# Strassen blocks for the up-projection of a gated MLP, with the down-projection as a phase of its own

## The chip, the cores and the metric

The kernel runs on one core of a Trainium2 chip. The metric is the device time of one execution in microseconds (us). Inputs and outputs lie in HBM; the work runs on TensorE (matrix products), VectorE, ScalarE and GpSimd (elementwise work), and on DMA queues, which SyncE issues here. TensorE's products accumulate in PSUM, and everything else lies in SBUF, 128 partitions wide. In the rows of the profile TensorE is PE, its weight load PEld, VectorE DVE, ScalarE ACT, GpSimd POOL and SyncE SP.

## The reference

One layer of a streaming encoder on 1024 tokens of 1024 channels, in float32. Only the last part is touched by the change:

```python
proj = einsum('btd,dc->btc', h, w_in)            # 1024 -> 2560 columns
mix = concat([pool_mixer(...), hgrn2_mixer(...)]) @ w_out
h = layer_norm(ALPHA * h + mix, ln1_g, ln1_b)    # 1024 tokens x 1024
u = einsum('btd,df->btf', h, w_up)               # 1024 -> 2 * 2816
uc = conv_b + sum(conv_w[j] * pad(u)[:, j:j + T] for j in range(3))
a, v = split(uc, 2)
ffn = einsum('btf,fd->btd', gelu(a) * v, w_down) # 2816 -> 1024
h = layer_norm(ALPHA * h + ffn, ln2_g, ln2_b)
```

## The kernel before

Every large product is done in three passes. An operand r is split into a high part h (a copy in the format F32R, by ScalarE) and a low part r - h (a subtraction, by VectorE): this is `split`, lines 66 to 68. `mm3` (lines 84 to 87) then issues three matmuls, high x high, high x low, low x high, into the same place of PSUM. Line 67 is thus every high part, line 68 every low part, and lines 85 to 87 nearly all matmuls. A matmul has a 128x128 stationary operand and a moving one of 128x512.

Weights come by `weight` (line 73): a DMA of 128x1024 values (512 KB) on SyncE's queue into one of three buffers `raw`, then a split into one of five pairs `wh`, `wl`. PSUM is cut into four units of 128x1024 (`unit`, line 56); each has two halves of 512 columns.

The kernel runs in stages: the input projection with the two mixers woven into it; the output projection with the first norm; the gated MLP; the second norm. The arrays `bh` and `bl` [channel, token] hold the operand of each stage in high and low parts, 8 channel tiles of 128 x 1024 tokens. The weights `w_out` with k from 5 on lie in a pool of their own (`woh`, `wol`).

**Output projection and first norm (lines 500 to 535).** Eight token tiles of 128 tokens: the first three share each arriving row of weights, the others follow one by one. For each tile VectorE adds the residual out of PSUM (line 530) and takes statistics (line 485), and `layer_norm` forms the normed state in `z[t]`, which stays in SBUF for the residual of the second norm. `hidden(t)` transposes the tile by eight TensorE transposes into a unit of PSUM (line 515), and ScalarE and VectorE write it as high and low part into `bh`, `bl` (lines 518, 519). The last two tiles are transposed inside the first feature block of the up-projection.

**Gated MLP (lines 542 to 620).** The 2816 features are 22 blocks f of 128. For a block, `up_pair` makes the a tile and the v tile of `w_up`, each as two token halves of 8 channel tiles x 3 matmuls. Then come the convolution over tokens (ScalarE's pass with scale and bias, line 550, and two steps of VectorE, line 554, for each of a and v), GELU, the product, and a split into `gh`, `gl`, which are the stationary operands of the down-projection. `down` takes a group of blocks (`GRP`: nine of two, one of four): for each of eight token tiles it adds up the group's blocks in PSUM, and VectorE adds the result to `z[t]` (lines 601, 603). The down-projection of a group is issued after the first block of the next group, so that TensorE has work while a group's gated blocks are made. The last group ends in the second norm (lines 591 and 608).

**What sets the order.** The framework gives each engine one queue, in which it places the instructions while building; their order can differ from that of the code, since an instruction that is ready early is moved forward. At run time each engine works its queue in order, and an instruction waits for semaphores of other engines or of DMA queues. A read or a write of a tile waits for what touched it last on another engine; a unit of PSUM is one tile, with both its halves.

Of the kernel before, what the change touches and what calls it, by code (L numbers as in the profile page):

```python
# [682 lines left out]
```

## Time and profile before

| | |
|---|---|
| time, median of 3 runs | 1122.4 us (1122.37 to 1122.55) |
| span of the profiled execution | 1121.3 us |
| its own time | not recorded apart from its span |
| mean granted TensorE clock | 0.997 |
| TensorE busy | 1108.6 us, 5076 matmuls in the trace |
| VectorE busy | 641.0 us |
| ScalarE busy | 301.4 us |
| moved by DMA | 65.65 MB |

The span runs from the first to the last instruction, the time of a run also covers what lies around it. A busy time is the union of an engine's instructions; where several matmuls are under way at once it counts them once. The granted clock is a share of TensorE's full speed, 2.4 GHz; 0.50 is its lower level of 1.2 GHz.

### The profile page before, as it was taken

To read this page: it belongs to the slowest core of one execution; us is meant where nothing else is said; L and a number is where in the kernel's file an instruction comes from. 1 tells how busy PE (TensorE), PEld (TensorE's weight loads), DVE (VectorE), ACT (ScalarE), POOL (GpSimd) and SP (SyncE) were. 2 spreads that over 40 slices of the span, in tenths; PEclk is the share of its full clock that TensorE was granted. 3 is DMA by queue.
4 is the path that set the end of the run, shared out by engine and by line. 5 is a ranking of instruction groups with operands and counts; after the bars stand their busy time and mean duration, and the time that the engine had idled before them with its cause. 6 is when DMAs were issued, how large, how long until landed. Compare 5 with 4: busy or idle time off the path is not lost.

```text
span 1121.3 us, 11896 instructions
## 1 busy us (share of the span) xinstructions
PE 1108.6 (99%) x5076; PEld 916.7 (82%) x5076; DVE 641.0 (57%) x668; ACT 301.4 (27%) x314; POOL 59.0 (5%) x71
## 2 busy tenths in 40 slices
PE   9999999999999999999999999999999999999996
PEld 7888888888888888888888888888888888888874
DVE  6585498677756744635354453535445453454388
ACT  5422433324500232122221212213131221313211
POOL 2000000011011100000000000000000000000025
PEclk9999999999999999999999999999999999999998
DMA  8200111101321411021111102111110211111012
GB/s 314 93 1 29 47 57 38 39 19 48 116 70 51 149 58 57 22 73 38 57 57 38 57 19 76 38 57 57 38 57 19 75 38 57 41 54 37 1 57 94
DMA packets 19205, 65.65 MB, mean 59 GB/s; under 512 B 2128, under 2 KB 3024, under 8 KB 19152
## 3 DMA queue, kind: packets, MB, share of 16 engines
q1 hardware_dynamic: 19008, 64.82, 17.4%
q8 instruction: 40, 0.66, 0.2%
q14 instruction: 13, 0.11, 0.0%
q10 hardware_dynamic: 144, 0.07, 0.0%
HBM read 60.68 MB, written 4.19 MB: 58 GB/s over the span
## 4 chain that ended last, share of the span: by engine, by line
PE 95%; POOL 2%; DVE 1%; ACT 0%; DMA 0%; issue 0%; POOLq 0%; DVEq 0%
PE u L85 30%; PE u L86 30%; PE u L87 30%; PE u L228 2%; POOL z L465 1%; POOL rs L448 1%; PE u L268 1%; PE u L515 1%; PE u L270 1%; PE u L257 1%; DVE z L480 0%; ACT z L462 0%; DVE st L485 0%; POOL rs L449 0%; PE u L195 0%; PE u L196 0%
## 5 line engine op out<-in xcount | busy, mean ns | idle before, releaser
L85 PE MATMUL u<-bh,wh 128*128 128x512 f32 x960 | 375.6, 392 | 0.6 <-ACT bh L67 0.6
L86 PE MATMUL u<-bl,wh 128*128 128x512 f32 x960 | 374.5, 390 | 0.0
L87 PE MATMUL u<-bh,wl 128*128 128x512 f32 x960 | 374.3, 390 | 0.0
L68 DVE TENSOR_TENSOR wl<-raw,wh 128x1024 fp32r<-128x1024 f32 x88 | 107.1, 1229 | 285.6 <-ACT wh L67 283.2
L85 PEld LDWEIGHTS u<-bh,wh 128*128 128x128 f32 x960 | 180.6, 188 | 38.4 <-ACT bh L67 1.1
L86 PEld LDWEIGHTS u<-bl,wh 128*128 128x128 f32 x960 | 180.7, 188 | 37.7 <-DVE bl L68 0.8
L87 PEld LDWEIGHTS u<-bh,wl 128*128 128x128 f32 x960 | 180.6, 188 | 37.8
L67 ACT ACTIVATE wh<-raw 128x1024 fp32r<-128x1024 f32 x88 | 92.1, 1059 | 389.0 <-PE u L86 259.2
L85 PE MATMUL u<-wh,gh 128*128 128x512 f32 x352 | 139.3, 396 | 0.0
L87 PE MATMUL u<-wh,gl 128*128 128x512 f32 x352 | 139.2, 396 | 0.0
L86 PE MATMUL u<-wl,gh 128*128 128x512 f32 x352 | 139.2, 395 | 0.0
L603 DVE TENSOR_TENSOR z<-u,z 128x1024 f32<-128x1024 f32 x64 | 78.3, 1224 | 57.5 <-PE u L87 57.5
L85 PEld LDWEIGHTS u<-wh,gh 128*128 128x128 f32 x352 | 66.1, 188 | 16.2 <-ACT gh L67 0.3
L86 PEld LDWEIGHTS u<-wl,gh 128*128 128x128 f32 x352 | 66.1, 188 | 16.0
L87 PEld LDWEIGHTS u<-wh,gl 128*128 128x128 f32 x352 | 66.1, 188 | 15.9
L554 DVE SCALAR_TENSOR_TENSOR cv<-u,pkt,cv 128x1023 f32<-128x1023 f32 (+4 forms) x46 | 56.7, 1232 | 9.3 <-ACT cv L550 8.8
L448 POOL TENSOR_SCALAR rs<-mv 128x1 f32<-128x1 f32 x16 | 17.5, 1093 | 799.0 <-DVE mv L456 799.0
L554 DVE SCALAR_TENSOR_TENSOR ca<-u,pkt,ca 128x1023 f32<-128x1023 f32 (+4 forms) x46 | 56.7, 1233 | 2.2 <-ACT ca L550 1.4
L85 PE MATMUL u<-wh,bh 128*128 128x512 f32 x144 | 57.6, 400 | 0.0
L86 PE MATMUL u<-wl,bh 128*128 128x512 f32 x144 | 56.2, 390 | 0.0
L87 PE MATMUL u<-wh,bl 128*128 128x512 f32 x144 | 56.2, 390 | 0.0
L67 ACT ACTIVATE gh<-ca 128x1024 fp32r<-128x1024 f32 (+1 forms) x23 | 23.6, 1025 | 104.4 <-DVE ca L578 104.4
(123 smaller groups left out, 949.1 us busy)
## 6 DMA issues: line engine op xcount, KB each, us to landing
raw<-in_w_up SPq DMA_DIRECT2D x44, 512.0 KB, 3.5
raw<-in_w_down SPq DMA_DIRECT2D x22, 512.0 KB, 3.5
raw<-in_w_ct SPq DMA_DIRECT2D x13, 512.0 KB, 3.4
raw<-in_w_out SPq DMA_DIRECT2D x8, 512.0 KB, 3.5
raw<-in_x SPq DMA_DIRECT2D x8, 512.0 KB, 3.9
hg<-in_xT SPq DMA_DIRECT2D x7, 512.0 KB, 8.1
out<-z SPq DMA_DIRECT2D x6, 512.0 KB, 2.6
raw<-in_w_i SPq DMA_DIRECT2D x4, 512.0 KB, 5.2
```

What stands on the lines that cost most here:

```text
L67: A.activation(out=h, in_=r, func=AF.Copy)
L68: V.tensor_tensor(out=l, in0=r, in1=h.bitcast(F32), op=ALU.subtract)
L85: PE.matmul(o, lhsT=ah, rhs=bh, start=start, stop=False)
L86: PE.matmul(o, lhsT=ah, rhs=bl, start=False, stop=False)
L87: PE.matmul(o, lhsT=al, rhs=bh, start=False, stop=stop)
L228: PE.matmul(ul[:, p * P:(p + 1) * P], lhsT=km[:, p * P:(p + 1) * P], rhs=view(QF, p * P + hh, [2 * hh, 64 // hh], [512 - hh, 2], [1, hh]), ...
L257: PE.matmul(up[:, c * P:(c + 1) * P], lhsT=KTr[:, c * P:(c + 1) * P], rhs=vchunk(c, hs), start=True, stop=True)
L268: PE.matmul(uo[:, cs], lhsT=vchunk(c, hs), rhs=sc[:, cs], start=True, stop=c == 0)
L270: PE.matmul(uo[:, cs], lhsT=S[:, (c - 1) * P:c * P], rhs=QF[:, cs], start=False, stop=True)
L448: G.tensor_scalar(out=rs, in0=mv[:, 1:2], scalar1=LN_EPS, scalar2=None, op0=ALU.add)
L554: V.scalar_tensor_tensor(out=c[:, o], in0=u[:, i], scalar=pkt[:, cw + j:cw + j + 1], in1=c[:, o], op0=ALU.mult, op1=ALU.add)
L603: V.tensor_tensor(out=z[t], in0=u, in1=z[t], op=ALU.add)
```

## The change

The first norm, the up-projection and the down-projection are rebuilt.

**The products.** For each feature block f the up-projection is a 2x2 block product: rows are the a tile and the v tile of the weights, the inner dimension is the two halves of the channels (four channel tiles each), and the columns are the two token halves. A form of Strassen's scheme makes it from seven block products of 4 channel tiles x 3 matmuls each: "11", "12", "s1", "s2", "s3", "22", "s4" (`pair`). Their weight operands are blocks of the weights or sums of them, formed in `prep` (two loads, four half-width sums, three full-width splits and one half-width split). Their token operands are the first token half as it is (in `bh`, `bl`), and for the second half four combinations T1 to T4 and B22, formed in `hidden` from the transposed tile t and the tile t - 4 of the first half, which is kept in `fh`. T1 and B22 lie in the second token half of `bh`, `bl`; T2, T3, T4 in new arrays `th`, `tlo`.

**The accumulation.** A block uses two units of PSUM with the halves c1, c2 and c3, c4. c1 takes "11", is copied by ScalarE, takes "s2" on top, is copied, takes "s3" on top, is copied. c3 takes "s1", is read, and takes "s4" on top. VectorE adds the copies to c2, c3 and c4 and so makes the tiles a and v in SBUF. `post` does the convolution, GELU and the product on these.

**The phases.** The up-projection of all 22 blocks comes first: in `step`, the block f, the convolution of block f - 1 and the weights of block f + 1 go side by side. The product goes to HBM (`gd`), and the normed state too (`hd`); the output projection takes the token tiles in the order 0, 4, 1, 5, 2, 3, 6, 7, and tile 6 is transposed ahead of the last channel tile of tile 7. Then the down-projection runs as a phase of its own, in groups of 2, 4, 4, 4, 4 and 4 blocks: weights and gated blocks are loaded and split, the latter into `bh`, `bl`, the former into `wh`, `wl` or, for f % 10 from 5 on, into the pairs `dh`, `dl` of a new pool. The second norm is as before.

The core of the diff (`parts` cuts a split weight into its two channel halves, `blocks` regards a transposed tile as 8 or 4 tiles of 128, `step` advances each generator; `first_group` brings the operands of the first group while the last block runs):

```diff
-GRP = (2,) * 9 + (4,)
+GRP = (2,) + (4,) * 5
...
+    hd = [tc.dram_tile([P, D], F32, name=f"hd{t}") for t in range(NC)]
+    gd = [tc.dram_tile([P, T], F32, name=f"gd{f}") for f in range(NF)]
+    tpp = tc.tile_pool(name="tpp", bufs=1, reuse_waits="tile")
+    tp = tpp.__enter__()
+    th, tlo = (tp.tile([P, 3, 4, 512], F32R, name=n) for n in ("th", "tlo"))
...
+    first_half = {}
     def hidden(t):
         ut = unit()
         for k in range(KT):
             PE.transpose(out=ut[:, k * P:(k + 1) * P], in_=z[t][:, k * P:(k + 1) * P], identity=identt)
-        ut3 = ut.rearrange("p (k t) -> p k t", t=P)
         ts = slice(t * P, (t + 1) * P)
-        A.activation(out=bh[:, :, ts], in_=ut3, func=AF.Copy)
-        V.tensor_tensor(out=bl[:, :, ts], in0=ut3, in1=bh[:, :, ts].bitcast(F32), op=ALU.subtract)
+        if t < 4:
+            split(blocks(ut), bh[:, :, ts], bl[:, :, ts])
+            r = zp.tile([P, 1024], F32, tag="fh", name="fh", bufs=2)
+            A.activation(out=r, in_=ut, func=AF.Copy)
+            first_half[t] = r
+            return
+        r = first_half.pop(t - 4)
+        d = rawp.tile([P, 1024], F32, tag="raw", name="rawd")
+        s = slice(ts.start - 512, ts.stop - 512)
+        V.tensor_tensor(out=d[:, lo], in0=r[:, lo], in1=ut[:, lo], op=ALU.subtract)
+        A.activation(out=r[:, lo], in_=ut[:, lo], func=AF.Copy)
+        V.scalar_tensor_tensor(out=d[:, hi], in0=ut[:, hi], scalar=-1.0, in1=d[:, lo], op0=ALU.mult, op1=ALU.subtract)
+        split(blocks(d[:, hi]), th[:, 0, :, s], tlo[:, 0, :, s])
+        split(blocks(d[:, lo]), bh[:, 0:4, ts], bl[:, 0:4, ts])
+        V.tensor_tensor(out=r[:, lo], in0=ut[:, hi], in1=r[:, lo], op=ALU.subtract)
+        split(blocks(r[:, lo]), th[:, 1, :, s], tlo[:, 1, :, s])
+        V.tensor_tensor(out=r[:, hi], in0=r[:, hi], in1=d[:, hi], op=ALU.add)
+        split(blocks(r[:, hi]), th[:, 2, :, s], tlo[:, 2, :, s])
+        split(blocks(ut[:, hi]), bh[:, 4:8, ts], bl[:, 4:8, ts])
+    def norm1(u, t):
+        z[t] = zp.tile([P, D], F32, tag="z", name="z")
+        nc.sync.dma_start(out=z[t], in_=x[t])
+        V.scalar_tensor_tensor(out=z[t], in0=z[t], scalar=ALPHA, in1=u, op0=ALU.mult, op1=ALU.add)
+        st6 = small.tile([P, 2, 6], F32, tag="st6", name="st6")
+        for c in halves:
+            stats(z[t], c, st6)
+        layer_norm(z[t], g1, b1_, st6, "whole", hd[t])
     late = []
-    for tl in ((0, 1, 2), (3,), (4,), (5,), (6,), (7,)):
+    for tl in ((0, 4, 1), (5,), (2,), (3,), (6,)):
         us = [unit() for t in tl]
         out_proj(us, tl)
-        while late and late[0] < tl[-1] - 1:
+        while len(late) > 1:
             hidden(late.pop(0))
         late += tl
         for u, t in zip(us, tl):
-            V.scalar_tensor_tensor(out=z[t], in0=xr, scalar=ALPHA, in1=u, op0=ALU.mult, op1=ALU.add)
-            layer_norm(z[t], g1, b1_, st6, "whole")
+            norm1(u, t)
+    hidden(late.pop(0))
+    u7 = unit()
+    out_proj([u7], (7,), (7, lambda: hidden(late.pop(0))))
+    norm1(u7, 7)
     wop.__exit__(None, None, None)
+    def prep(f):
+        ra, rv = raw(w_up[f]), raw(w_up[NF + f])
+        w = wpair()
+        split(ra, *w)
+        o = ops[f] = {}
+        o["11"], o["12"] = parts(w)
+        yield
+        s1 = ua.tile([P, 512], F32, tag="s1", name="s1")
+        V.tensor_tensor(out=s1, in0=rv[:, lo], in1=rv[:, hi], op=ALU.add)
+        V.tensor_tensor(out=rv[:, lo], in0=ra[:, lo], in1=rv[:, lo], op=ALU.add)
+        yield
+        V.tensor_tensor(out=ra[:, lo], in0=s1, in1=ra[:, lo], op=ALU.add)
+        V.tensor_tensor(out=ra[:, hi], in0=ra[:, lo], in1=ra[:, hi], op=ALU.add)
+        yield
+        w = wpair()
+        split(ra, *w)
+        o["s2"], o["s4"] = parts(w)
+        yield
+        w = wpair()
+        split(rv, *w)
+        o["s3"], o["22"] = parts(w)
+        yield
+        o["s1"] = [ua.tile([P, 512], F32R, tag=f"w1{n}", name=f"w1{n}", bufs=1) for n in "hl"]
+        split(s1, *o["s1"])
+    def prod(o, w, b, start, stop):
+        for k in range(4):
+            ks = slice(k * P, (k + 1) * P)
+            mm3(o, w[0][:, ks], w[1][:, ks], b[0][:, k, :], b[1][:, k, :], start and k == 0, stop and k == 3, skip_group_check=True)
+    def block(k, n):
+        return [e[:, k * 4:(k + 1) * 4, halves[n]] for e in (bh, bl)]
+    B11, T1, B21, B22 = block(0, 0), block(0, 1), block(1, 0), block(1, 1)
+    T2, T3, T4 = [[e[:, i] for e in (th, tlo)] for i in range(3)]
+    def pair(f):
+        w = ops[f]
+        a, v = outs[f] = [ua.tile([P, T], F32, tag=f"u{n}", name=f"u{n}") for n in "av"]
+        u = unit()
+        c1, c2 = u[:, lo], u[:, hi]
+        prod(c1, w["11"], B11, True, False)
+        A.activation(out=a[:, lo], in_=c1, func=AF.Copy)
+        yield
+        prod(c2, w["12"], B21, True, True)
+        V.tensor_tensor(out=a[:, lo], in0=c2, in1=a[:, lo], op=ALU.add)
+        yield
+        prod(c1, w["s2"], T2, False, False)
+        A.activation(out=a[:, hi], in_=c1, func=AF.Copy)
+        yield
+        u = unit()
+        c3, c4 = u[:, lo], u[:, hi]
+        prod(c3, w["s1"], T1, True, False)
+        yield
+        prod(c1, w["s3"], T3, False, True)
+        A.activation(out=v[:, lo], in_=c1, func=AF.Copy)
+        V.scalar_tensor_tensor(out=v[:, hi], in0=c3, scalar=-1.0, in1=v[:, lo], op0=ALU.mult, op1=ALU.subtract)
+        yield
+        prod(c4, w["22"], T4, True, True)
+        V.tensor_tensor(out=v[:, lo], in0=c4, in1=v[:, lo], op=ALU.subtract)
+        yield
+        prod(c3, w["s4"], B22, False, True)
+        V.tensor_tensor(out=a[:, hi], in0=c3, in1=a[:, hi], op=ALU.add)
...
+    def post(f):
+        a, v = outs.pop(f)
+        cv, ca = (ug.tile([P, T], F32, tag=f"c{n}", name=f"c{n}") for n in "va")
+        conv(cv, v, NF + f)
+        yield
+        yield
+        conv(ca, a, f)
+        yield
+        A.activation(out=ca, in_=ca, func=AF.Gelu_apprx_tanh)
+        yield
+        V.tensor_tensor(out=ca, in0=ca, in1=cv, op=ALU.mult)
+        nc.sync.dma_start(out=gd[f], in_=ca)
+    preps = [prep(f) for f in range(NF)]
+    step([preps[0]], 6)
+    step([preps[1]])
+    pairs = [pair(0), pair(1)]
+    step(pairs[:1], 2)
+    step(pairs[1:])
+    hidden(7)
+    step(pairs[1:])
     g2, b2 = row(2, "g"), row(3, "b")
...
+    step([pairs[0], preps[1]], 6)
+    step([pairs[1], post(0), preps[2]], 6)
+    for f in range(2, NF - 1):
+        step([pair(f), post(f - 1), preps[f + 1]], 7)
+    def down_weight(f):
+        if f % 10 < 5:
+            wd[f] = weight(w_down[f])
+            return
+        r = raw(w_down[f])
+        wd[f] = [dn.tile([P, 1024], F32R, tag=f"d{n}", name=f"d{n}") for n in "hl"]
+        split(r, *wd[f])
+    def gated(f):
+        r = raw(gd[f])
+        split(r, bh[:, f % 8, :], bl[:, f % 8, :])
...
+    for p in (post(NF - 2), post(NF - 1)):
+        step([p], 6)
+    tpp.__exit__(None, None, None)
+    zq = ctx.enter_context(tc.tile_pool(name="zq", bufs=1, reuse_waits="tile"))
+    dn = ctx.enter_context(tc.tile_pool(name="dn", bufs=5, side="right", reuse_waits="tile"))
+    z = [zq.tile([P, D], F32, name=f"z{t}") for t in range(NC)]
+    for t in range(NC):
+        nc.sync.dma_start(out=z[t], in_=hd[t])
+    for gi, fs in enumerate(groups):
+        last = gi == len(groups) - 1
+        ahead = [] if last else list(groups[gi + 1])
         for t in range(NC):
             ts = slice(t * P, (t + 1) * P)
-            last = gi == len(GRP) - 1
...
-                for i, (gh, gl) in enumerate(gs):
-                    mm3(u[:, c], gh[:, ts], gl[:, ts], ws[i][0][:, c], ws[i][1][:, c], i == 0, i == len(gs) - 1)
+                for f in fs:
+                    mm3(u[:, c], bh[:, f % 8, ts], bl[:, f % 8, ts], wd[f][0][:, c], wd[f][1][:, c], f == fs[0], f == fs[-1])
                 if last and t >= SPLIT:
                     drain(u, c)
             if not last:
                     V.scalar_tensor_tensor(out=z[t], in0=z[t], scalar=ALPHA, in1=u, op0=ALU.mult, op1=ALU.add)
                 else:
                     V.tensor_tensor(out=z[t], in0=u, in1=z[t], op=ALU.add)
+                if ahead:
+                    f = ahead.pop(0)
+                    down_weight(f)
+                    gated(f)
```

**Order of TensorE's queue in the middle of the up-projection.** `u_...` are units of PSUM. Before, one block (`u_3151` is its a tile, `u_3152` its v tile) and the first rows of the next one behind it:

```order
L85 MATMUL u_3151<-bh_82,wh_3141 128x512 [waits DVE_49]
L86 MATMUL u_3151<-bl_83,wh_3141 128x512
L87 MATMUL u_3151<-bh_82,wl_3142 128x512
...
L85 MATMUL u_3152<-bh_82,wh_3147 128x512 [waits DVE_49]
...
L85 MATMUL u_3275<-bh_82,wh_3265 128x512 [waits DVE_49]
...
L85 MATMUL u_3276<-bh_82,wh_3271 128x512 [waits DVE_49,Activation_49]
```

After, one block (`u_3416` holds c1 and c2, `u_3477` c3 and c4; `w1h` is the high part for s1), with the next block's first unit `u_3547`; each row left out belongs to the product of the row above it:

```order
L85 MATMUL u_3416<-bh_82,wh_3308 128x512 [waits Activation_49]
...
L85 MATMUL u_3477<-bh_82,w1h_3397 128x512
...
L85 MATMUL u_3416<-th_2017,wh_3360 128x512 [waits DVE_49]
...
L85 MATMUL u_3477<-bh_82,w1h_3397 128x512
...
L85 MATMUL u_3547<-bh_82,wh_3439 128x512
L85 MATMUL u_3416<-th_2017,wh_3380 128x512 [waits Activation_49]
...
L86 MATMUL u_3547<-bl_83,wh_3439 128x512
...
L85 MATMUL u_3477<-th_2017,wh_3380 128x512 [waits DVE_49]
...
L87 MATMUL u_3547<-bh_82,wl_3440 128x512
...
L85 MATMUL u_3477<-bh_82,wh_3360 128x512 [waits DVE_49]
...
L85 MATMUL u_3547<-bh_82,wh_3439 128x512 [waits Activation_49]
```

Before, one wait stood in front of 48 matmuls of one accumulation. Now the products of a block alternate with those of its other unit and of the next block, and five rows of a block wait for VectorE or ScalarE.

**Order of VectorE's queue between output projection and up-projection.** `wl_2624` and `wl_2630` are the low parts of the first a and v tile of `w_up`, `z6` and `z7` the last two token tiles. Before:

```order
L68 TENSOR_TENSOR wl_2624<-raw_2621,wh_2623 128x1024 [waits DMAHW6_49,Activation_49]
L476 SCALAR_TENSOR_TENSOR z6_1991<-z6_1991,mv_2530,row0_1996 128x1024 [waits DVE_49]
L68 TENSOR_TENSOR wl_2630<-raw_2627,wh_2629 128x1024 [waits DMAHW7_49,Activation_49]
L480 SCALAR_TENSOR_TENSOR z6_1991<-z6_1991,rs_2532,row1_1998 128x1024 [waits DVE_49,Pool_49]
...
L530 SCALAR_TENSOR_TENSOR z7_1992<-raw_2597,u_2537 128x1024 [waits DMAHW5_49,PE_49]
L519 TENSOR_TENSOR bl_83<-u_2586,bh_82 128x8x128 [waits Activation_49]
L485 BN_STATS st6_2600<-z7_1992 128x6 [waits DVE_49]
L485 BN_STATS st6_2600<-z7_1992 128x6
L68 TENSOR_TENSOR wl_2894<-raw_2891,wh_2893 128x1024 [waits DMAHW2_49,Activation_49]
```

After (`wl_2717` is the low part of the first a tile, `u_2663` the transposed tile 6, `z_2694` the token tile 7):

```order
L547 TENSOR_TENSOR rawd_2672<-fh_2591,u_2663 128x512 [waits PE_49,Activation_49]
L549 SCALAR_TENSOR_TENSOR rawd_2672<-u_2663,rawd_2672 128x512 [waits Activation_49]
L68 TENSOR_TENSOR bl_83<-rawd_2672,bh_82 128x4x128 [waits Activation_49]
L552 TENSOR_TENSOR fh_2591<-u_2663,fh_2591 128x512
L68 TENSOR_TENSOR tlo_2018<-rawd_2672,th_2017 128x4x128 [waits Activation_49]
L554 TENSOR_TENSOR fh_2591<-fh_2591,rawd_2672 128x512
L561 SCALAR_TENSOR_TENSOR z_2694<-z_2694,u_2620 128x1024 [waits DMAHW3_49,DMAHW0_49,PE_49]
L68 TENSOR_TENSOR tlo_2018<-fh_2591,th_2017 128x4x128 [waits Activation_49] x2
L68 TENSOR_TENSOR bl_83<-u_2663,bh_82 128x4x128 [waits Activation_49]
L498 BN_STATS st6_2697<-z_2694 128x6 [waits DVE_49]
L498 BN_STATS st6_2697<-z_2694 128x6
L68 TENSOR_TENSOR wl_2717<-raw_2712,wh_2716 128x1024 [waits DMAHW5_49]
```

The low part of the first weight stood among the norms of tile 6; now it stands behind the nine half-width operations of the transposed tile 6, the residual add of tile 7 and its statistics.

**Order of SyncE's queue at the end of the up-projection.** Before, with loads for both projections in alternation:

```order
L63 DMA raw_5495<-in_w_up 128x1024 [waits DMAHW3_49,DVE_49]
L63 DMA raw_5501<-in_w_up 128x1024 [waits DMAHW4_49,DVE_49]
L63 DMA raw_5619<-in_w_down 128x1024 [waits DMAHW5_49,DVE_49]
L63 DMA raw_5625<-in_w_down 128x1024 [waits DMAHW6_49,DVE_49]
L63 DMA raw_5743<-in_w_up 128x1024 [waits DMAHW7_49,DVE_49]
```

After (`gd20` and `gd21` are the last two gated blocks, `hd` the normed state in HBM):

```order
L674 DMA gd20_2012<-ca_5626 128x1024 [waits DVE_49]
L63 DMA raw_5734<-in_w_down 128x1024 [waits DMAHW5_49,DVE_49]
L63 DMA raw_5740<-gd4_1996 128x1024 [waits DMAHW7_49,DMAHW2_49,DVE_49]
L737 DMA z0_5656<-hd0_1984 128x1024 [waits PE_49]
L737 DMA z1_5657<-hd1_1985 128x1024 [waits Pool_49]
...
L737 DMA z7_5663<-hd7_1991 128x1024 [waits DMAHW2_49]
L674 DMA gd21_2013<-ca_5637 128x1024 [waits DMAHW3_49,DVE_49]
L63 DMA raw_5758<-in_w_down 128x1024 [waits DMAHW4_49,Activation_49]
```

The loads of the normed state stand as one run of eight between the stores of the last two gated blocks, and in front of the loads for the groups that follow.

## Rows read from the trace of the kernel before

**Rows 1.** The page: busy time, share, instructions; then the chain of waits by engine.

```profile
PE 1108.6 (99%) x5076; PEld 916.7 (82%) x5076; DVE 641.0 (57%) x668; ACT 301.4 (27%) x314; POOL 59.0 (5%) x71
...
PE 95%; POOL 2%; DVE 1%; ACT 0%; DMA 0%; issue 0%; POOLq 0%; DVEq 0%
```

**Rows 2.** Stretches: us, busy (x) of PE, PEld, DVE, ACT, POOL; clock, DMA share, GB/s.

```profile
600.00:700.00 100.00, 100.00 (x440) 82.17 (x439) 45.68 (x39) 23.36 (x22) 0.00 (x0) 1.00 0.17 53
```

**Rows 3.** Groups by line, shapes apart: busy us, mean ns of one | idle before, releasers.

```profile
L85 PE MATMUL u<-bh,wh 128*128 128x512 f32 x960 | 375.6, 392 | 0.6 <-ACT bh L67 0.6
...
L68 DVE TENSOR_TENSOR wl<-raw,wh 128x1024 fp32r<-128x1024 f32 x88 | 107.1, 1229 | 285.6 <-ACT wh L67 283.2 <-PE u L228 2.4
...
L67 ACT ACTIVATE wh<-raw 128x1024 fp32r<-128x1024 f32 x88 | 92.1, 1059 | 389.0 <-PE u L86 259.2 <-PE u L87 122.0 <-DMA raw<-in_w_up 6.0
...
L554 DVE SCALAR_TENSOR_TENSOR cv<-u,pkt,cv 128x1022 f32<-128x1022 f32 x21 | 26.9, 1279 | 0.4
...
L240 DVE TENSOR_TENSOR hg<-hg,hg 128x512 f32<-128x512 f32 x28 | 19.2, 687 | 19.9 <-PE u L228 19.7
...
L591 DVE TENSOR_TENSOR z<-u,z 128x512 f32<-128x512 f32 x16 | 10.5, 678 | 0.7 <-PE u L87 0.7
...
L302 ACT ACTIVATE tmp<-u 128x512 f32<-128x512 f32 x8 | 4.4, 590 | 0.2 <-PE u L87 0.2
...
L554 DVE SCALAR_TENSOR_TENSOR ca<-u,pkt,ca 128x512 f32<-128x512 f32 x2 | 1.5, 751 | 1.5 <-ACT ca L550 1.4
```

**Rows 4.** Timeline from 600 us: start, us, engine, line, operation [idle before, releaser].

```profile
599.84 0.40 PE L87 MATMUL u<-wh,gl 128*128 128x512 f32 x1
...
601.24 0.40 PE L87 MATMUL u<-wh,gl 128*128 128x512 f32 x1
...
601.67 1.23 DVE L603 TENSOR_TENSOR z<-u,z 128x1024 f32<-128x1024 f32 x1 [1.57 <-PE u L87]
...
605.64 0.39 PE L85 MATMUL u<-bh,wh 128*128 128x512 f32 x1
...
615.16 0.39 PE L85 MATMUL u<-bh,wh 128*128 128x512 f32 x1
```

**Rows 5.** Timeline from 384 us, VectorE behind the output projection.

```profile
384.40 1.22 DVE L519 TENSOR_TENSOR bl<-u,bh 128x1024 fp32r<-128x1024 f32 x1
...
385.53 1.28 DVE L485 BATCH_NORM_STATS2 st<-z 128x6 f32<-128x512 f32 x2
...
386.72 1.21 DVE L68 TENSOR_TENSOR wl<-raw,wh 128x1024 fp32r<-128x1024 f32 x1
```

**Rows 6.** Timeline from 388 us: TensorE starting again, and the last transposed tile.

```profile
388.88 0.19 PEld L85 LDWEIGHTS u<-bh,wh 128*128 128x128 f32 x1
...
389.22 0.40 PE L86 MATMUL u<-bl,wh 128*128 128x512 f32 x1
...
395.52 1.03 ACT L518 ACTIVATE bh<-u 128x1024 fp32r<-128x1024 f32 x1 [5.30 <-PE u L515]
...
396.58 1.23 DVE L519 TENSOR_TENSOR bl<-u,bh 128x1024 fp32r<-128x1024 f32 x1 [4.04 <-ACT bh L518]
...
396.60 0.30 PEld L85 LDWEIGHTS u<-bh,wh 128*128 128x128 f32 x2 [0.39 <-ACT bh L518]
```

**Rows 7.** Stretches of 1 us at the end, with columns as in rows 2.

```profile
1110.00:1111.00 1.00, 0.21 (x1) 0.00 (x0) 0.97 (x3) 0.00 (x0) 0.92 (x2) 1.00 0.94 381
1114.00:1115.00 1.00, 0.00 (x0) 0.00 (x0) 1.00 (x2) 0.00 (x0) 1.00 (x1) 0.92 0.55 209
1115.00:1116.00 1.00, 0.00 (x0) 0.00 (x0) 0.80 (x1) 0.00 (x0) 0.92 (x3) 0.50 0.15 53
```

**Rows 8.** Timeline from 0 us: matmuls before the clock is up.

```profile
7.81 0.63 PE L86 MATMUL u<-bl,wh 128*128 128x512 f32 x1
...
8.24 0.63 PE L87 MATMUL u<-bh,wl 128*128 128x512 f32 x1
```

**Rows 9.** The page: DMA issues, count, KB each, median us from issue to landing.

```profile
raw<-in_w_down SPq DMA_DIRECT2D x22, 512.0 KB, 3.5
```

More of the change, by code (lines that the diff above doesn't have):

```diff
@@ L498, in out_weight, with out_proj @@
         return h, l
-    def out_proj(us, tl):
+    def out_proj(us, tl, at=None):
         for k in range(KT):
+            if at is not None and k == at[0]:
+                at[1]()
             if w_rows[k] is None:
@@ L582, in down, with parts @@
-    def down(gi, fs, gs):
-        ws = [weight(w_down[f]) for f in fs]
+            norm1(u, t)
[3 more added lines that the diff above has]
+    norm1(u7, 7)
+    wop.__exit__(None, None, None)
+    uap = tc.tile_pool(name="uap", bufs=2, side="right", reuse_waits="tile")
+    ua = uap.__enter__()
+    ops, outs = {}, {}
+    lo, hi = halves
+    def parts(w):
+        return [[e[:, c] for e in w] for c in halves]
+    def prep(f):
[22 more added lines that the diff above has]
+        split(s1, *o["s1"])
@@ new lines, in conv @@
+    def conv(c, u, ft):
+        cw = PK_CW + 3 * ft
+        A.activation(out=c, in_=u, func=AF.Identity, scale=pkt[:, cw + 2:cw + 3], bias=pkt[:, PK_CB + ft:PK_CB + ft + 1])
+        for j in (1, 0):
+            V.scalar_tensor_tensor(out=c[:, 2 - j:], in0=u[:, :T - 2 + j], scalar=pkt[:, cw + j:cw + j + 1], in1=c[:, 2 - j:], op0=ALU.mult, op1=ALU.add)
+    def post(f):
[10 more added lines that the diff above has]
+        nc.sync.dma_start(out=gd[f], in_=ca)
@@ new lines, in step @@
+    def step(gens, n=1):
+        for i in range(n):
+            for g in gens:
+                next(g, None)
+    preps = [prep(f) for f in range(NF)]
[6 more added lines that the diff above has]
+    step(pairs[1:])
+    zpp.__exit__(None, None, None)
+    ugp = tc.tile_pool(name="ugp", bufs=2, reuse_waits="tile")
+    ug = ugp.__enter__()
+    g2, b2 = row(2, "g"), row(3, "b")
+    step([pairs[0], preps[1]], 6)
@@ new lines, in block_kernel @@
+    step([pairs[1], post(0), preps[2]], 6)
+    for f in range(2, NF - 1):
+        step([pair(f), post(f - 1), preps[f + 1]], 7)
+    groups, f0 = [], 0
+    for n in GRP:
+        groups.append(list(range(f0, f0 + n)))
+        f0 += n
+    wd = [None] * NF
+    def down_weight(f):
[5 more added lines that the diff above has]
+        split(r, *wd[f])
@@ new lines, in gated, with first_group @@
+    def gated(f):
+        r = raw(gd[f])
+        split(r, bh[:, f % 8, :], bl[:, f % 8, :])
+    def first_group():
+        for f in groups[0]:
+            down_weight(f)
+            yield
+        for i in range(3):
+            yield
+        for f in groups[0]:
+            gated(f)
+            yield
+    step([pair(NF - 1), first_group()], 7)
+    for p in (post(NF - 2), post(NF - 1)):
+        step([p], 6)
+    ugp.__exit__(None, None, None)
+    tpp.__exit__(None, None, None)
+    uap.__exit__(None, None, None)
```

72 lines of the change are left out of this document (12 added, 60 removed).

## The prediction

> **What bounds the kernel now.** I read the busy table first: TensorE is busy for 99% of the span, VectorE for 57%, ScalarE for 27%, and the chain of waits that ended last lies on TensorE for 95% [rows 1]. The table of stretches says the same of the MLP: in a stretch of 100 us that holds both projections TensorE never rests, VectorE works 46 us and ScalarE 23 us, the DMA engines are used to 17%, at the full granted clock, the upper of its two levels, 2.4 GHz [rows 2]. So a matmul taken out is time taken out, unless the engines that feed it come late. The size of the gain is not in the table of groups, though: its mean of 392 ns for a matmul [rows 3] is from entry to exit, and several are under way at once. The timeline gives what one costs. In the up-projection the starts at 605.64 and 615.16 lie 42 matmuls apart: 0.2267 us each [rows 4]. In the down-projection the starts at 599.84 and 601.24 lie six apart: 0.2333 us [rows 4].
>
> **Matmuls.** A feature block (one a tile and one v tile; there are 22) takes 2 tiles x 2 token halves x 8 channel tiles x 3 = 96 matmuls now, and 7 products x 4 x 3 = 84 after. The down-projection keeps its 48 per block. Which pitch holds for the new operands no row shows. In the built programs the operands of the slower rows (gh, gl) start 32 bytes past a multiple of 64, those of the faster ones (wh, wl, bh, bl) on a multiple. By that, as an estimate, the s1 product (12 of 84, weights w1h, w1l) and the down weights dh, dl (10 of 22 blocks) run at 0.2333, the rest, th and tlo too, at 0.2267. Before: 22 x 96 x 0.2267 + 22 x 48 x 0.2333 = 478.8 + 246.4 = 725.2 us. After: 22 x (72 x 0.2267 + 12 x 0.2333) + 480 x 0.2333 + 576 x 0.2267 = 420.7 + 242.6 = 663.3. That is **-61.9 us**; -47.7 if all ran at the slower pitch, -66.9 if all at the faster. The transposes stay 64.
>
> **The work beside it.** Per block VectorE gets three full-width splits (1229 ns), one half-width split and four half-width sums (687), three adds out of PSUM (678) and one scalar_tensor_tensor (751), four taps of the convolution (1279) and the product (1.22 as a split): 16.3 us by durations [rows 3]. Neighbours overlap: starts at 384.40, 385.53 and 386.72 are 1.13 apart for a full-width operation of 1.22 and 1.19 for two half-width ones of 0.64 [rows 5], about 0.09 less for each of 17 operations: 14.7 us. A block lasts 84 matmuls, 19.1 us, so VectorE fits, with 4 us to spare. ScalarE has 8.5 full-width passes, at the 1059 ns of a high part [rows 3] 9 us. The 60 added transfers of 512 KB land in about 3.5 us each [rows 9] on DMA engines that are mostly free, and weights are loaded a block ahead. All this is hidden as long as the order of the queues fits, which is the next point.
>
> **Four short waits in each block.** Both halves of a unit of PSUM count as one tile: s2 waits until VectorE has read c2, s3 until ScalarE has copied c1, 22 until VectorE has read c3 (after ScalarE's copy), s4 until it has read c4. The built order puts matmuls of other products into these gaps: 9, 4, 7 and 4. The lags, from rows: a matmul ends 0.39 after it starts; the reader starts 0.03 later (601.24 + 0.40, then 601.67) [rows 4]; after ScalarE's end at 396.55 VectorE starts at 396.58 and TensorE at 396.60 [rows 6]; a pipeline that was stopped takes 0.34 from the first weight load to the second matmul (388.88 to 389.22), 0.11 more than the pitch [rows 6]. Counted from the start of the last matmul before the gap:
> - s4: 0.39 + 0.03 + 0.68 + 0.05 = 1.15 against 5 pitches, 1.13: with the restart 0.13 late.
> - 22: 0.39 + 0.03 + 0.59 (half-width ScalarE copy [rows 3]) + 0.03 + 0.75 + 0.05 = 1.84 against 8 pitches, 1.81: 0.14 late.
> - s3: 1.06 against 1.15: in time.
> - s2: the read of c2 stands in VectorE's queue behind seven operations. Counted from the last matmul of 22 of the block before: 1.10 (the read of c4) + 1.13 (split) + 0.2 (ScalarE's pass) + 3 x 1.19 (taps) + 2 x 0.60 (sums) + 0.59 + 0.68 = 8.5. TensorE arrives after 1.13 + 0.13 (s4), 24 x 0.2267 and 9 x 0.2333, at 8.8. In time, by 0.3.
>
> Sum 0.27 a block, some 20 blocks: **+6**. No row shows such a loop. Below, 0: the order covers all. Above: VectorE at its full durations ends the read of c2 0.6 later and one late wait pushes the next, 1.2 a block, 26 us. I take 6, since each term is nearest to the rows in which nothing else runs.
>
> **From the output projection to the up-projection.** Now VectorE does 1.2 us for each transposed tile after the first norm; after, a tile of the second token half costs it nine half-width operations, each behind a ScalarE pass. In the new order tile 6 is transposed six matmuls before the output projection ends. Behind it in VectorE's queue stand those nine, the residual add of tile 7 and two statistics, and only then the low split of the first up weight. Added up with the ScalarE passes between them, from the end of the transposes: 2.2 for two sums with ScalarE's copy between, 2.4 for two low splits and two sums, 1.1 for the add, 1.8 for three low splits, 1.2 for the statistics, 1.2 for the weight's own split: the low part is there at 9.9. ScalarE's high part is there at 4.0. TensorE has six matmuls (1.4 us) and two more from 4.0 on: idle for 2.7 + 5.4 = 8.1 us. Then c2 waits for the copy of c1 (0.85, nothing stands between), pair 1 for its high weight at the end of three ScalarE passes behind VectorE's last sum (2.8), and its own c2 again 0.85. Together 12.6 us; before, TensorE waited 0.4 there [rows 6]. In the idle 5.4 us the clock may fall: after the last matmul (to 1110.21) the granted clock is still 0.92 in 1114 to 1115 and 0.50, the lower level of 1.2 GHz, from 1115 [rows 7]. Matmuls at that level start 0.43 apart (7.81, 8.24) [rows 8]; ten of them cost 2.0 more, of which the 2.8 us of waiting for pair 1 hide nearly all. I take **+13**. Bounds: 8 (nothing but the low split is late) and 17 (the clock stays low for the two next products).
>
> **From the up- to the down-projection.** The normed state comes back from HBM into the room of th and tlo, so its first load waits for product 22 of the last block. In SP's queue it stands behind two loads (wd4, gd4) and the store of gd20, which wait for VectorE, but ahead of the store of gd21. It is issued 0.2 us after that product, lands 3.5 later, and is needed only when the fifth token tile wants a free unit of PSUM, 11 us on. Added up the same way from the last product of block 20, the gated blocks 2 to 5 are split by 42 us, and TensorE comes for the last at 43. That is close; I add **+1** for the order of 22 and v, which waits behind a split (0 to 5).
>
> **The end.** The last group still has four blocks and the same norms; VectorE comes to it without the splits of the last gated block: **-0.5** (-2 to 0).
>
> **Sum.** -61.9 + 6 + 13 + 1 - 0.5 = -42.4. The profiled execution has a span of 1121.3 and the runs a median of 1122.4; what lies around the span (1.1) stays, so the change is taken off the median: **1080 us**.
>
> **Rivals.**
> 1. The loops bind. VectorE works at its full durations, the wait for c2 becomes the longest of each block, 26 us instead of 6: 1100. For it: VectorE goes from 46% busy to nearly 80%, in order, with ScalarE in the loop. Against it: 4 us to spare per block.
> 2. Nothing is late but the first low split: 0 for the loops, 8 for the first join, 0 for the second: 1068. For it: the order was laid so that other products fill each gap. Against it: sums of rows exceed two of the four gaps.
> 3. Slower than before: the short stops bring the clock down. If in a block all 84 matmuls started 0.43 apart, it would cost 84 x 0.203 = 17.1 us; from 2.5 of the 22 blocks on, the 42 us are gone, and with every other block it is 1080 + 11 x 17.1 = 1268 us. Against it: the granted clock is full for 4 us after the last matmul [rows 7], and these stops are a fifth of a microsecond. The Trainium skill ("TensorE: Matmul & The Clock Gate", section "A second HAM failure mode: psum-queue depth-cycling") says that frequent micro-idles between groups of matmuls, while units of PSUM are cycled, can make the clock oscillate; by that rule the change loses, and no run here shows stops of this kind.
>
> That the matmuls are not removed is excluded: TensorE's program has 4461 rows instead of 4726.
>
> **How the numbers follow.** The forecast has 0.54 (its own range 1072 to 1091), rival 1 0.23, rival 2 0.17, rival 3 0.05; 0.01 is left for sums of delays that just meet the gain. The range goes from rival 2 to a little beyond rival 1: 1066 to 1105. A measurement tells 0.2% from no change, 2.2 us, which only the last two cases come near: faster 0.94, same 0.01, slower 0.05.
>
> **What would show it.** Right: 1848 up matmuls in the trace; a pitch of 0.227 inside a product; blocks of 19.3 to 19.7 us; one hole of 7 to 10 us on TensorE near 385, ended by the low split of the first up weight, and some 3 us soon after; full clock in the up-projection; no wait for the loads of z. Wrong: blocks above 20.3 us (rival 1); a granted clock of 0.50 in the up-projection (rival 3); an idle TensorE at the second join, ended by a DMA or by a split of a gated block.

## The result and the profile after

The changed kernel takes 1082.1 us (median of 4 runs, 1081.6 to 1083.2) against 1122.5 us for the kernel before: a ratio of 0.964, 95% interval 0.963 to 0.965. The forecast was 1080, with 1072 to 1091 as its own range.

The page's busy times, and the chain of waits by engine, for [rows 1]:

```profile
PE 1059.0 (98%) x4812; PEld 863.7 (80%) x4812; DVE 761.6 (70%) x882; ACT 387.3 (36%) x444; POOL 57.0 (5%) x71
...
PE 91%; DVE 3%; POOL 2%; ACT 1%; DMA 1%; issue 1%; POOLq 0%; DVEq 0%; ACTq 0%
```

TensorE still sets the end; it has 264 matmuls fewer, and VectorE 121 us more work. The stretches (columns as in [rows 2]) show where TensorE is not busy:

```profile
385.00:390.00 5.00, 0.73 (x2) 0.30 (x2) 5.00 (x9) 2.81 (x5) 0.00 (x0) 0.85 0.30 105
390.00:395.00 5.00, 2.73 (x7) 2.18 (x8) 5.00 (x8) 0.63 (x1) 1.99 (x2) 0.50 0.00 0
395.00:405.00 10.00, 8.51 (x38) 6.10 (x36) 8.77 (x12) 4.69 (x7) 0.00 (x0) 0.98 0.60 211
440.00:780.00 340.00, 340.00 (x1466) 270.79 (x1465) 266.50 (x298) 153.26 (x176) 0.00 (x0) 1.00 0.25 81
```

From 385 to 395 us, between output projection and up-projection, TensorE is busy for 3.5 us while VectorE never rests, and the granted clock goes to its lower level, 0.50. From 440 to 780 TensorE counts as busy all the time at the full clock, and VectorE has 266.5 of 340 us, 78%.

The first join in the timeline (start, length, engine, line, operation, idle time before and what ended it):

```profile
383.41 0.39 PE L87 MATMUL u<-woh,bl 128*128 128x512 f32 x1
...
386.22 0.50 PE L85 MATMUL u<-bh,wh 128*128 128x512 f32 x1 [2.42 <-ACT wh L67]
...
386.56 0.40 PE L86 MATMUL u<-bl,wh 128*128 128x512 f32 x1
...
391.00 1.21 DVE L68 TENSOR_TENSOR wl<-raw,wh 128x1024 fp32r<-128x1024 f32 x1
...
392.27 0.80 PE L87 MATMUL u<-bh,wl 128*128 128x512 f32 x1 [5.31 <-DVE wl L68]
392.86 0.63 PE L85 MATMUL u<-bh,wh 128*128 128x512 f32 x1
...
394.99 0.55 PE L87 MATMUL u<-bh,wl 128*128 128x512 f32 x1
...
396.93 0.50 PE L85 MATMUL u<-bh,wh 128*128 128x512 f32 x1 [0.69 <-ACT ua L635]
...
400.73 0.50 PE L85 MATMUL u<-bh,wh 128*128 128x512 f32 x1 [0.77 <-ACT wh L67]
...
405.63 0.50 PE L85 MATMUL u<-bh,wh 128*128 128x512 f32 x1 [0.35 <-ACT ua L635]
```

These are the waits of the forecast, in its order: the high part of the first weight, its low part, the copy of c1, the high part of the next block's weight, the copy again.

A block of the up-projection (L649 reads c3, L652 reads c4, L638 reads c2; the matmuls with th at 451.60 and 463.08 begin 22 and s2, the one at 455.41 begins s4):

```profile
450.85 0.69 DVE L649 SCALAR_TENSOR_TENSOR uv<-u,uv 128x512 f32<-128x512 f32 x1 [0.67 <-ACT uv L648]
...
451.37 0.39 PE L86 MATMUL u<-bl,wh 128*128 128x512 f32 x1
...
451.60 0.49 PE L85 MATMUL u<-th,wh 128*128 128x512 f32 x1
...
454.66 0.69 DVE L652 TENSOR_TENSOR uv<-u,uv 128x512 f32<-128x512 f32 x1 [3.12 <-PE u L87]
...
455.14 0.39 PE L87 MATMUL u<-bh,wl 128*128 128x512 f32 x1
...
455.41 0.50 PE L85 MATMUL u<-bh,wh 128*128 128x512 f32 x1
455.74 0.39 PE L86 MATMUL u<-bl,wh 128*128 128x512 f32 x1
...
457.35 0.39 PE L87 MATMUL u<-bh,wl 128*128 128x512 f32 x1
457.58 0.39 PE L85 MATMUL u<-bh,wh 128*128 128x512 f32 x1
...
462.06 0.69 DVE L638 TENSOR_TENSOR ua<-u,ua 128x512 f32<-128x512 f32 x1
...
463.08 0.39 PE L85 MATMUL u<-th,wh 128*128 128x512 f32 x1
```

The stops are too short to count as idle time. They show in the spacing: 0.27 ahead of 455.41, and 0.33 after 451.60 and after 455.41 (the next starts are 451.93 and 455.74), where the pitch, the distance of two starts in an unbroken stream, is 0.23. The seven distances from 455.74 to 457.35 are 0.230 on average, and from there it is 0.227 again. The read of c2 ends at 462.75, 0.33 before s2 begins. The next s4 begins at 474.91: the block lasts 19.5 us.

The second join in the timeline, and the DMA issues of z (count, KB each, median us to landing), beside [rows 9]:

```profile
826.04 0.39 PE L85 MATMUL u<-wh,bh 128*128 128x512 f32 x1
...
826.83 1.37 SPq L737 DMA_DIRECT2D z<-hd  x3
...
827.09 0.50 PE L85 MATMUL u<-bh,wh 128*128 128x512 f32 x1 [0.66 <-DVE uv L652]
```

```profile
z<-hd SPq DMA_DIRECT2D x8, 512.0 KB, 8.8
```

One wait of 0.66 us for the read of c4, of the size forecast; no other follows. The loads of z land in 8.8 us (median), not in 3.5, and are still in time.

### The profile page after: what moved, and what is told of

The parts are those of the page before. It is cut to its first block, busy times and chain, and to the rows that moved or that the text cites. A ratio compares the mean times of both kernels' runs of the same rounds, so it can differ in the third digit from the quotient of the medians.

```text
span 1080.3 us, 11913 instructions
## 1 busy us (share of the span) xinstructions
PE 1059.0 (98%) x4812; PEld 863.7 (80%) x4812; DVE 761.6 (70%) x882; ACT 387.3 (36%) x444; POOL 57.0 (5%) x71
## 4 chain that ended last, share of the span: by engine, by line
PE 91%; DVE 3%; POOL 2%; ACT 1%; DMA 1%; issue 1%; POOLq 0%; DVEq 0%; ACTq 0%
PE u L85 29%; PE u L86 28%; PE u L87 28%; PE u L228 2%; POOL z L478 1%; POOL rs L461 1%; PE u L268 1%; PE u L535 1%; DVE z L493 1%; PE u L270 1%; PE u L257 1%; DVE st L498 1%; DMA raw<-gd 0%; ACT z L475 0%; ACT wh L67 0%
## 5 line engine op out<-in xcount | busy, mean ns | idle before, releaser
L85 PE MATMUL u<-bh,wh 128*128 128x512 f32 x520 | 208.0, 401 | 5.4 <-ACT wh L67 3.2
L87 PE MATMUL u<-bh,wl 128*128 128x512 f32 x520 | 204.7, 394 | 5.3 <-DVE wl L68 5.3
L86 PE MATMUL u<-bl,wh 128*128 128x512 f32 x520 | 204.2, 393 | 0.0
L86 PE MATMUL u<-wl,bh 128*128 128x512 f32 x336 | 131.4, 391 | 0.0
L85 PEld LDWEIGHTS u<-bh,wh 128*128 128x128 f32 x520 | 98.6, 190 | 33.7 <-DVE uv L652 7.4
L87 PEld LDWEIGHTS u<-bh,wl 128*128 128x128 f32 x520 | 98.4, 189 | 27.0 <-DVE wl L68 6.0
L86 PEld LDWEIGHTS u<-bl,wh 128*128 128x128 f32 x520 | 98.5, 189 | 19.7 <-DVE bl L68 0.4
L85 PE MATMUL u<-th,wh 128*128 128x512 f32 x264 | 105.4, 399 | 0.0
L87 PE MATMUL u<-th,wl 128*128 128x512 f32 x264 | 103.5, 392 | 0.0
L86 PE MATMUL u<-tlo,wh 128*128 128x512 f32 x264 | 103.2, 391 | 0.0
```

The costliest lines, as they stand in the source:

```text
L85: PE.matmul(o, lhsT=ah, rhs=bh, start=start, stop=False, **kw)
L86: PE.matmul(o, lhsT=ah, rhs=bl, start=False, stop=False, **kw)
L87: PE.matmul(o, lhsT=al, rhs=bh, start=False, stop=stop, **kw)
```

## The experiments

Each run stood beside the kernel before on the same chip; ratios are to that kernel (the changed kernel: 0.964).

**e1: the phases without the seven products.** `pair` does the four plain products, `prep` two splits, `hidden` one split for each tile:

```diff
-        prod(c1, w["11"], B11, True, False)
...
+        for n, ns in enumerate(halves):
+            for u, w in zip(us, ops[f]):
+                for k in range(KT):
...
+                    mm3(u[:, ns], w[0][:, ks], w[1][:, ks], bh[:, k, ns], bl[:, k, ns], k == 0, k == KT - 1)
```

> The phases, the stores and the loads of the gated blocks and of the normed state stay as in the changed kernel; the seven products are put back to the four plain ones (2112 matmuls in the up-projection, no sums, no added passes over token tiles). Theory (the gain is the matmuls taken out; the phases cost nothing): as before, less 576 of the down-projection's matmuls that read faster operands (576 x 0.0067 = 3.9 us), less 1.6 at the tail, plus 1 at the second join: 1118 us, within 1113 to 1124. Rival (the phases or the trips through HBM cost or gain something of their own, hidden in the sum): above 1128 or below 1108.

Measured: 1128.3 us, ratio 1.0045 (1.0031 to 1.0059): outside the theory's range and just inside the rival's. Its timeline has one hole, at the second join:

```profile
873.11 4.95 SPq L670 DMA_DIRECT2D z<-hd  x8
...
881.25 0.80 PE L85 MATMUL u<-wh,bh 128*128 128x512 f32 x1 [6.46 <-DVE z L691]
```

Here the loads of z stand behind four more loads and the last store in SyncE's queue, and the residual add that frees a unit of PSUM is late. Spacing beyond the pitch, hole and the slow matmuls behind it, adds up to 9.6 us; taken off by calculation, they leave 1118.7, near the theory's 1118. So away from that join the phases and the trips through HBM cost nothing that shows, but the second join is hidden only by where these loads stand, and the rival is right that it can cost. With the plain products nothing is gained, so the gain of the change is that of the matmuls.

**e2: each half of a unit a tile of its own.**

```diff
-        u = unit()
-        c1, c2 = u[:, lo], u[:, hi]
+        c1, c2 = half(), half()      # [P, 512], eight of them; c3, c4 and tile 7 alike
```

> Each half of a unit of PSUM is a tile of its own in the up-projection, so that only the waits remain which the data ask for. Theory (the four short stops cost 0.27 us a block and are due to both halves counting as one tile): 20 x 0.27 = 5.4 us less, 1076.7 us (1075 to 1079). Rival (the block's period of 19.5 us is set by the loop over VectorE and ScalarE, and the stops are only where that shows): 1082 us, within 1081 to 1083.

Measured: 1073.4 us, 0.9557 (0.9544 to 0.9570), some 9 us less than the changed kernel, where 5.4 were expected. The same stretch as above has 1495 matmuls instead of 1466:

```profile
440.00:780.00 340.00, 340.00 (x1495) 280.30 (x1494) 268.06 (x302) 156.34 (x177) 0.00 (x0) 1.00 0.26 84
```

The block goes from 19.51 to 19.13 us, which is 84 matmuls at their pitch with no stop left: the stops cost 0.38 us a block, not 0.27. Of this, 0.25 stands at 22 (0.10) and s4 (0.15), where it was forecast, and 0.04 at s3; most of the rest is behind the stops. In the changed kernel, over the 34 stops of 0.33 from 440 to 780 us, the next nine starts are 0.2296 apart on average, and from the tenth on it is 0.2267. Over the blocks that is some 8 us; the wait at the second join is gone as well, and the first join costs the same in sum. The rival falls: with the same VectorE work the block is shorter.

The run changes more than the waits: the built order now gives the seven products one after the other, where the changed kernel alternates them. The alternation by itself is not the cost: in the changed kernel TensorE goes from a row with th at 454.23 to one of another product at 454.46, without a wait, at the usual 0.227.

**e3 and e8: the right side of SBUF moved by 32 bytes**, in the changed kernel and in the kernel before:

```diff
+    padp = ctx.enter_context(tc.tile_pool(name="padp", bufs=1, side="right"))
+    padt = padp.tile([P, 8], F32, name="padt")
+    V.memset(padt, 0.0)
     wop = tc.tile_pool(name="wop", bufs=1, side="right", reuse_waits="tile")
```

> A tile of 32 bytes ahead of the pools on the right side of SBUF moves w1h, w1l, dh, dl and the last three rows of w_out onto multiples of 64 bytes; nothing else is changed. Theory (the pitch of 0.2333 instead of 0.2267 goes with operands that start 32 bytes past such a multiple): (264 + 480 + 144) x 0.0067 = 5.9 us less, 1076.2 us (1075 to 1078). Rival (the slower pitch goes with the operand's role or its side of SBUF): 1082 us, within 1081 to 1083.

> The kernel before with the tile of 32 bytes ahead of the pools on the right side: gh, gl and the last three rows of w_out come to multiples of 64 bytes. Theory (pitch by place): (1056 + 144) x 0.0067 = 8.0 us less, 1115 us against 1123 (1113.5 to 1116.5). Rival (the slower pitch belongs to the down-projection's operands, not to their place): 1123 us.

Measured: e3 1077.1 us, 0.9590 (0.9577 to 0.9603), 5.6 us less by the ratio; e8 1116.4, 0.9939 (0.9925 to 0.9952), which is 6.9 us. The pitch does go with the place. In the changed kernel the matmuls of s1 were 0.2333 apart (three in 0.70):

```profile
519.48 0.39 PE L85 MATMUL u<-bh,w1h 128*128 128x512 f32 x1
...
520.18 0.40 PE L85 MATMUL u<-bh,w1h 128*128 128x512 f32 x1
...
520.88 0.40 PE L85 MATMUL u<-bh,w1h 128*128 128x512 f32 x1
...
521.58 0.39 PE L85 MATMUL u<-th,wh 128*128 128x512 f32 x1
```

After the move they are 0.2267 apart:

```profile
440.96 0.39 PE L85 MATMUL u<-bh,w1h 128*128 128x512 f32 x1
...
441.64 0.39 PE L85 MATMUL u<-bh,w1h 128*128 128x512 f32 x1
...
442.32 0.39 PE L85 MATMUL u<-bh,w1h 128*128 128x512 f32 x1
```

From 840 to 1050 us the mean spacing goes from 0.2308 to 0.2267. In e8 the stretch of [rows 2] holds 442 matmuls instead of 440:

```profile
600.00:700.00 100.00, 100.00 (x442) 82.79 (x442) 44.65 (x37) 24.25 (x23) 0.00 (x0) 1.00 0.16 53
```

Part of the gain is lost elsewhere: in both runs the end of the span comes 1.0 us later behind the last matmul (12.5 us against 11.5 in e8), where the chain that ended last runs over the last norms, and in e3 the lower clock lasts longer at the first join.

**e4: the first weight split ahead of tile 6.**

```diff
-    out_proj([u7], (7,), (7, lambda: hidden(late.pop(0))))
+    out_proj([u7], (7,), (7, lambda: (next(preps[0]), hidden(late.pop(0)))))
```

> The first a tile of w_up is split before tile 6 is transposed, so that its low part stands ahead of the nine operations in VectorE's queue. Theory of the prediction (TensorE's hole at the first join is ended by this low part): the 2.6 and 5.5 us go, 1074 us. Rival, which I hold the likelier now (the hole is filled by whatever is late next: the chain norm of tile 7, its transposes, its nine operations, which the products with T1 and T2 need; in the changed kernel these came to VectorE at 402.8 and TensorE used the last of them without idling at 408.5, and the products of the first token half are only 48 matmuls, 10.9 us): the wait moves behind these products, 1079 to 1083 us.

Measured: 1083.4 us, 0.9646 (0.9633 to 0.9659): no gain. The two holes of 2.42 and 5.31 us are gone, and one of 9.11 stands behind the first two products of block 0:

```profile
390.11 0.39 PE L87 MATMUL u<-bh,wl 128*128 128x512 f32 x1
...
396.60 2.95 ACT L67 ACTIVATE wh<-raw 128x1024 fp32r<-128x1024 f32 x3 [5.43 <-DVE raw L587]
...
399.60 0.79 PE L85 MATMUL u<-bh,wh 128*128 128x512 f32 x1 [9.11 <-ACT wh L67]
```

The rival holds in its result (to 0.4 us), not in its chain: what is late next is not tile 7 but the first weight of block 1, third of three passes of ScalarE that wait for VectorE's sums.

**e5: tile 6 ahead of tile 3.**

```diff
-    for tl in ((0, 4, 1), (5,), (2,), (3,), (6,)):
+    for tl in ((0, 4, 1), (5,), (2,), (6,), (3,)):
```

> The output projection takes the token tiles in the order 0, 4, 1, 5, 2, 6, 3, 7 instead of 0, 4, 1, 5, 2, 3, 6, 7: behind its end VectorE has the nine half-width operations for tile 7 alone, and for tile 3 one split. Theory A (VectorE's amount of work behind the output projection sets the hole; it is busy all the time from 385 to 395 us): 9 x 0.60 less 1.13 = 4.3 us less, 1078 us (1076 to 1079.5). Theory B (the chain of tile 7 alone sets it: norm, transposes, nine operations): 1082 us, within 1081 to 1083.

Measured: 1079.6 us, 0.9614 (0.9600 to 0.9627), 2.9 us less by the ratio. Theory A has the direction, and two thirds of its size; the time is just outside its range. The longest wait left, 4.23 us, is again for the first weight of block 1.

**e6, e7, e9: more work for VectorE in each block**, behind the gated product (once, and five times) or on the convolved v tile (once):

```diff
         V.tensor_tensor(out=ca, in0=ca, in1=cv, op=ALU.mult)
+        V.scalar_tensor_tensor(out=ca, in0=dum, scalar=0.0, in1=ca, op0=ALU.mult, op1=ALU.add)
```

> One more full-width operation of VectorE in each block, on the gated product (it adds zero times a constant tile), which the built order puts behind the low part of s1, where VectorE has 0.35 us and then 0.67 us of idle time before it reads c3. Theory (VectorE's work is hidden as long as its queue lets it read PSUM in time): 22 x 0 to 0.15 us more, 1084 us (1082 to 1087). Rival (VectorE's load is near its limit, so each operation costs): 22 x 1.2 = 26 us more, 1108 us.

> The same added operation, but on the convolved v tile: the built order puts it two places ahead of the read of c2, on which s2 waits; in the changed kernel that read ends 0.28 us before s2 would begin. Theory (the place in the queue decides, not the share of busy time): 1.19 less 0.28, and 0.1 for the restart, 1.0 us a block, 20 to 22 us more, 1103 us (1097 to 1109). Rival (4 us of idle time a block hide it wherever it stands): 1082 to 1085 us.

> Five more full-width operations of VectorE in each block, on the gated product. VectorE has 15.2 us of work in a block of 19.5; one more of it cost nothing in either of the two runs that added one. Theory (VectorE hides up to some 4 us and sets the block from there): 15.2 + 5 x 1.2 = 21.2 us a block, 1.7 more, 22 x 1.7 = 37 us more, 1119 us (1107 to 1130). Rival (its idle time lies in waits for PSUM that cannot be filled, so that it binds much earlier): 15.2 + 6.0 + about 3 of such waits, 24.2 us a block, 103 us more, 1185 us.

Measured: e6 1080.5 us, 0.9619 (0.9606 to 0.9632); e7 1082.1, 0.9634 (0.9621 to 0.9647); e9 1115.3, 0.9929 (0.9915 to 0.9942). One more operation costs nothing, five cost 33 us, of which some 27 lie in the blocks (22 x 1.2) and most of the rest at the second join, where TensorE waits 3.97 and 3.71 us for residual adds. In e6 the operation stands where it was expected, but the built order of TensorE's rows changed with it, so its zero is that of both. My expectation of e7 was wrong, and the run does not test it: the framework placed the added operation ahead of the read of c2 in every second block only (from 490 us on), and there laid other matmuls of TensorE in front of s2. Whether the place alone would cost 1 us a block stays open. In e9 VectorE sets the block, 20.7 us, and TensorE stops visibly for the read of c2:

```profile
440.00:780.00 340.00, 325.40 (x1388) 257.81 (x1388) 337.03 (x360) 142.81 (x163) 0.00 (x0) 1.00 0.21 76
```

```profile
507.05 0.39 PE L87 MATMUL u<-bh,wl 128*128 128x512 f32 x1
...
507.46 0.68 DVE L638 TENSOR_TENSOR ua<-u,ua 128x512 f32<-128x512 f32 x1
...
508.19 0.50 PE L85 MATMUL u<-th,wh 128*128 128x512 f32 x1 [0.75 <-DVE ua L638]
```

**e10 and e11: the edits that gained, together** (e2, e3 and e5), and then the first split of block 1 ahead of block 0's sums:

```diff
-    step([preps[0]], 6)
-    step([preps[1]])
+    step(preps[:2])              # block 1 loads its v tile one step later
+    step([preps[0]], 5)
```

> The three edits that gained alone, together: each half of a unit a tile of its own (9.3 us less by its ratio), the right side moved by 32 bytes (5.6 less), tile 6 ahead of tile 3 (2.9 less). Theory (they are in three separate places, so the gains add up): 17.8 us less than the changed kernel, 1064.5 us (1062.5 to 1066.5). Rival (the two joins take back part of it, since TensorE comes to them earlier): 1068 to 1071 us.

> As the run of the three edits, and the first split of block 1 (its products 11 and 12) ahead of the sums and splits of block 0. With tile 6 ahead of tile 3 the longest hole, 4.2 us, was ended by the high part of this weight, third in a row of three passes of ScalarE behind VectorE's sums. Theory (that hole goes, and tile 7's nine operations are in time for the products with T1 and T2): 3 to 4.5 us less than the run of the three edits, 1061 us (1059 to 1063). Rival (the products with T1 and T2 wait instead): 1063.5 to 1066 us.

Measured: e10 1064.0 us, 0.9473 (0.9460 to 0.9486); e11 1059.0, 0.9424 (0.9412 to 0.9437). The gains add up, and e11 gains 4.9 us more, where 3 to 4.5 were expected. In its profiled run the first join has two waits left, 0.75 and 1.82 us, and the granted clock stays at 1.00 (h is a half of a unit, a tile of its own):

```profile
380.00:395.00 15.00, 14.25 (x72) 11.60 (x70) 14.88 (x19) 6.73 (x8) 2.04 (x2) 1.00 0.38 125
395.00:410.00 15.00, 13.15 (x57) 10.32 (x56) 13.48 (x21) 8.12 (x13) 0.00 (x0) 1.00 0.35 119
```

```profile
383.53 0.50 PE L95 MATMUL h<-bl,wh 128*128 128x512 f32 x1 [0.75 <-DVE bl L77]
...
397.19 0.49 PE L94 MATMUL h<-bh,w1h 128*128 128x512 f32 x1 [1.82 <-ACT bh L76]
```

The profiled run is the shortest of the four: 1057.3 us at a mean granted clock of 0.997; the others take 1059.0 to 1059.3 us at 0.995. So the clock may have come down in those, and no trace of them shows where.

## Why the prediction was right

| term | forecast, us | found, us | from |
|---|---|---|---|
| matmuls | -61.9 | about -61 | pitches as forecast in the up-projection; the down-projection 0.2308 instead of 0.2297, 1.2 more |
| stops in the blocks | +6 | about +8 | spacing beyond the pitch, 406 to 810 us; 20 x 0.38 by e2 |
| first join | +13 | +12.7 | spacing beyond the pitch, 383 to 406 us |
| second join | +1 | +0.9 | 0.82, and 0.10 at the restart |
| end | -0.5 | -1.6 | last start to end of span: 11.5 before, 9.9 after |
| sum | -42.4 | about -41 | spans: 1121.3 and 1080.3, -41.0 |

- **Matmuls.** The step held, and e1 shows that nothing else gains: with the plain products the phases alone are no faster than the kernel before. The guess at the pitch of operands that no row showed was right too, and e3 and e8 tested it.
- **Work beside it.** VectorE has 15.3 us in a block (266.5 x 19.5 / 340) where 14.7 were worked out; the forecast's 4 us to spare are there: 1.2 more are hidden (e6, e7), 6.0 are not (e9).
- **The four stops.** Which ones are late was right: 22 and s4, 0.10 and 0.15; s2 in time; s3, forecast in time, is 0.04 late. The size was short by about 2 us: the forecast counted a restart as over after one matmul, but the next nine are wider apart as well.
- **First join.** The size was right, and the waits came as listed: 2.42, 5.31, 0.69, 0.77 and 0.35, the fourth shorter than the 2.8 forecast because the matmuls at the lower clock filled it. In spacing beyond the pitch the five are 10.5 us; the matmuls at the lower clock add 1.5 and the restarts 0.7. The reason was too narrow. The low part of the first weight ended the hole but was not its price (e4). The runs point to VectorE's whole queue behind the output projection: shortening it (e5) and putting both first weights early in it (e11) is what gains.
- **Second join.** Right in size, with less cover than thought: the loads were slower and later than forecast, and in e1, with another place in the queue, 6.5 us come into the open.
- **The end.** It is 1.1 us shorter than forecast; no run tests why. With the matmuls (+0.9) and the stops (+2) this makes misses of both signs, which partly cancel in the sum.
- **Rivals.** The first needs blocks above 20.3 us; they last 19.5, and only five operations more bring it about. The second needs stops that cost nothing; e2 says 0.38. The third did not come: the stops in each block, and in e9 stops of 0.75 us, leave the granted clock at 1.00 from 440 to 780. The Trainium skill ("TensorE: Matmul & The Clock Gate", section "A second HAM failure mode: psum-queue depth-cycling") tells of another kernel in which frequent micro-idles between groups of matmuls, with PSUM cycled, made the clock oscillate. The traces of this kernel show no such oscillation at stops of 0.1 to 0.75 us.

## What to carry to other kernels

Where TensorE is busy for 99%, the price of a scheme that saves matmuls is the waits it puts between them, and these can be added up from the lags of single rows: how long after its last matmul a unit of PSUM is read, and how many other matmuls stand in the gap. Two tiles that share one tracked buffer wait for each other's readers; give each half its own. At a join, the instruction that ends the hole need not be its price: move it, and see whether the hole moves too.
